# The causal mask of the diagonal score blocks: a minimum on VectorE behind the exponential in place of a matmul ahead of it

## The chip, the cores and the metric

The kernel runs on one core of a Trainium2 chip. The metric is the device time of one execution in microseconds (us); before the change it is 3023.98 us, the median of three runs (3017.05 to 3034.43). The engines are named as in the profile: PE is TensorE's matmuls, PEld its weight loads, DVE is VectorE, ACT is ScalarE, POOL is GpSimd, SP the engine that issues most DMAs. Each engine works through its own queue in order; between engines, semaphores hold an instruction until what it needs is there.

## The reference

One inference step of a small hybrid decoder: a recurrent layer, one shared set of keys, values and log-forget sums, then an attention layer. It is computed for a prompt of 2048 new tokens and, with a paged cache, for 8 sequences of 8 tokens each ("decode" below). The change touches the prompt's attention alone, with 16 heads of 64:

```python
def fox_block(q, k, v, cq, ck, q_pos, k_pos):
    s = jnp.einsum('bqhd,bkhd->bhqk', q, k).astype(jnp.float32) * (HEAD_DIM ** -0.5)
    s = s + jnp.swapaxes(cq, 1, 2)[:, :, :, None] - jnp.swapaxes(ck, 1, 2)[:, :, None, :]
    mask = k_pos[None, :] <= q_pos[:, None]
    s = jnp.where(mask[None, None], s, -jnp.inf)
    p = jax.nn.softmax(s, axis=-1)
    return jnp.einsum('bhqk,bkhd->bqhd', p.astype(v.dtype), v)
```

A key that comes after the query must get the weight zero.

## The kernel before, in words

The program goes through the recurrent layer, the projections, the prompt's attention and the output projection. The attention (from about 1757 to 2825 us in the profile) runs beside most of the decode sequences, whose cached keys and values come in by DMA; the two are interleaved by a fixed share of estimated costs (`Side.along`).

The attention's work is cut into 64 units: a head and a block of 512 queries (`units`, four query blocks `qc` for each of 16 heads). A unit has 4(qc+1) score blocks, each with 128 keys (on the partitions) by 512 queries. For each score block:

- Two matmuls write the scores into a PSUM bank `st`: one with `ka` (L1592), one with `kbt` (L1593), which also brings in the forget sums and the row maximum.
- The last four blocks of a unit lie on the diagonal. Queries ahead of the block's keys are left out (`lo`), and the first 128 remaining columns need a triangular mask. Before the change a third matmul adds it (L1595): the identity in bfloat16 as weights (`identB`) by a fixed tile that holds 0 and -1e30 (`causal`).
- ACT takes the exponential into an SBUF tile (L1601), `acc` for a unit's first block and `p` for the others. There are 5 `acc` and 6 `p` tiles.

After every four blocks a group of product matmuls multiplies these tiles with the values (`product`, L1612, into `ops`). It is called two score blocks later (`later.after(2, product)`), and its first matmul is tied to the last entry of `pair`, the last of the four exponentials (`together`). POOL then adds each `p` to `acc` (line L108, a helper that many operations share), from which the row sums come; a `p` tile is free again when its product matmuls and this addition have read it.

The row maximum for a unit is worked out some units ahead: PE computes the scores once more into one of three banks `sx` (L1431), DVE takes their maximum (L1433; on the diagonal L1435, with a mask tile `maskb`) and frees the bank, PE transposes the maxima (`mps`, L1448), ACT writes them into `qbt` (L1450). DVE also transposes the decode's keys (`ktr`, L1180) and works on decode scores. Decode's matmuls are `dS` (L1148) and `dO` (L1262).

The code's order is not the order of the queues. The layer that builds the program places each instruction in its engine's queue by its own estimate of times, so removing or adding an instruction can move others.

Of the kernel before, what the change touches and what calls it, by code (L numbers as in the profile page):

```python
# [11 lines left out]
F32 = mybir.dt.float32  # L12
F32R = mybir.dt.float32r
I32 = mybir.dt.int32
AF = mybir.ActivationFunctionType
ALU = mybir.AluOpType
# [4 lines left out]
P = 128  # L21
# [10 lines left out]
NEG = -1.0e30  # L32
# [55 lines left out]
def tile_hawk_fox(  # L88
# [8 lines left out]
    V, A, G, T, S = nc.vector, nc.scalar, nc.gpsimd, nc.tensor, nc.sync  # L97
# [9 lines left out]
    def tt(eng, out, a, b, op):  # L107
        eng.tensor_tensor(out, a, b, op=op)  # L108
# [12 lines left out]
    def together(mms, after=(), beside=False):  # L121

        first = mms[0]().ins
        for d in after:
            tc.add_manual_dep(first, d.ins.name, SYNC)
        if beside:
            behind("T", first)
        with tc.high_priority(), tc.issue_after(first):
            for mm in mms[1:]:
                mm()  # L130
# [66 lines left out]
    def ct(name, shape, dtype=F32):  # L197
        return const.tile(shape, dtype, name=name, tag=name)

    ident = ct("ident", [P, P])  # L200
# [21 lines left out]
    def sbuf(es, name, side=None):  # L222
        return es.enter_context(tc.tile_pool(name=name, bufs=1, side=side, reuse_waits="tile"))
# [1110 lines left out]
    def attention(es):  # L1334
        pool = sbuf(es, "att")
# [15 lines left out]
        for i in range(NQ):  # L1351
            if i % 3 == 0 and i < 6:
                kb = kbs[i // 3]
                G.memset(f(kb[64:P, :]), 0.0)
                G.memset(f(kb[96:100, :]), 1.0)
            qb = qbs[i]
            G.memset(f(qb[64:P, :]), 0.0)
            G.memset(f(qb[64:67, :]), 1.0)
            if i == 0:
                G.memset(maskb[:, :], 0.0)  # L1360
                G.affine_select(maskb[:, :], maskb[:, :], pattern=[[-1, 512]], compare_op=ALU.is_ge, fill=NEG, base=384,
                                channel_multiplier=1)

        identB, causal = (pool.tile([P, P], mybir.dt.bfloat16, name=n) for n in ("identB", "causal"))
        V.tensor_copy(identB[:, :], ident[:, :])
        G.memset(causal[:, :], 0.0)
        G.affine_select(causal[:, :], causal[:, :], pattern=[[1, P]], compare_op=ALU.is_ge, fill=NEG, base=0,
                        channel_multiplier=-1)

        sel = pool.tile([P, 4, P], F32R, name="sel16")  # L1370
        rr = pool.tile([P, 512], F32R, name="r16")
# [23 lines left out]
        def load_keys(h):  # L1395
            kb = kbs[h % 2]
            loaded.add(h)
            for lo, hi in halves(h):
                queue[0].dma_start(f(kb[0:64, lo:hi]), kd_d[h * HD:(h + 1) * HD, 1, lo:hi])
                queue[0].dma_start(f(kb[64:67, lo:hi]), nc_d[h, :, lo:hi])  # L1400
# [55 lines left out]
        def finish(u, ops, acc):  # L1456
            h, qc = units[u]
            pr, h2 = divmod(h, 2)
            if u % 8 == 0:
                oTs_["sums"] = pool.tile([P, 32], F32, name="sums", tag="sums", bufs=2)  # L1460
            sums = oTs_["sums"]
            if h2 == 0:
                oTs_[qc] = pool.tile([P, 512], F32, name="oT", tag="oT", bufs=5)
            oT = oTs_[qc][h2 * HD:(h2 + 1) * HD, :].rearrange("d (a r c) -> d a r c", a=2, r=2)
            for r in range(2):
                A.copy(oT[:, :, r, :], ops[r * HD:(r + 1) * HD, :].rearrange("d (a c) -> d a c", a=2))
            accs.append((qc, acc))
            if len(accs) == 4 or h == H - 1:
                later.after(2, lambda todo=accs[:]: total(h2, sums, todo, h >= H - 2))
                accs.clear()  # L1470
            if u >= len(units) - 4:
                later.after(5, lambda oT=[oTs_[qc]]: norm(pr, sums, qc, 1, oT))
            elif u % 8 == 7:
                later.after(5, lambda oT=[oTs_[c] for c in range(4)]: norm(pr, sums, 0, 4, oT))
# [54 lines left out]
        start = [sum(nks[:u]) for u in range(len(units))]  # L1529
        done = [0, 0, 0]  # L1530

        def advance(tick):

            need = 0
            for u in range(len(units)):
                need = max(need, start[u] + nks[u] - 2 * max(0, start[u] - min(LEAD, RAMP + tick) - tick))
                if start[u] > tick + 40:
                    break
            while done[0] < min(need, len(tasks)):
                u, j, ck = tasks[done[0]]  # L1540
                while done[1] <= min(u + 1, len(units) - 1):
                    load_unit(done[1])
                    done[1] += 1
                top(u, j, ck)
                done[0] += 1
# [12 lines left out]
        pair = []  # L1558
        wide = [0]

        def scores_bank():

            if dec_done:
                wide[0] += 1
                if wide[0] % 2:
                    return psum["dec"].tile([P, 512], F32, name="st", tag="do"[wide[0] // 2 % 2], bufs=1)
            return ps3.tile([P, 512], F32, name="st", tag="st", bufs=2)
# [3 lines left out]
        def loads():  # L1571
            while lows[0] < len(units):
                v = lows[0]
                if tick < (start[v - 2] if v < 4 else min(max(start[v - 2], start[v - 3] + AFT), start[v] - 3)):
                    break
                with paged():
                    load_low(v)
                lows[0] += 1
            h, k = divmod(tick, 40)
            if k == 16 and h + 1 < H:  # L1580
                with paged():
                    load_head(h + 1)

        for u, (h, qc) in enumerate(units):
            for k in range(nks[u]):
                loads()
                ka, kb = heads[h], kbs[h % 2]
                qa, qb = qas[u], qbs[u % NQ]
                lo = max(0, k - qc * 4) * P
                ks = slice(k * P, (k + 1) * P)  # L1590
                ps = scores_bank()
                place["T"] = T.matmul(ps[:, lo:], ka[:, ks], qa[:, lo:], start=True, stop=False).ins  # L1592
                T.matmul(ps[:, lo:], kb[:, ks], qb[:, lo:], start=False, stop=(k < qc * 4))  # L1593
                if k >= qc * 4:
                    T.matmul(ps[:, lo:lo + P], identB[:, :], causal[:, :], start=False, stop=True)  # L1595
                done[2] = u + (k == nks[u] - 1)
                if k == 0:
                    p = acc = pool.tile([P, 512], F32, name="acc", tag="acc", bufs=NACC)
                else:
                    p = pool.tile([P, 512], F32, name="p", tag="p", bufs=NP)  # L1600
                pair.append((k, lo, p, A.activation(p[:, lo:], ps[:, lo:], AF.Exp)))  # L1601

                def product(u=u, h=h, todo=pair, acc=acc, last=(k == nks[u] - 1)):


                    nonlocal ops
                    if todo[0][0] == 0:
                        ops = ops2[:, u % 2 * 256:u % 2 * 256 + 256]

                    def mm(k, lo, p, r):  # L1610
                        a0 = (lo // P + 1 - r) // 2
                        return T.matmul(ops[r * HD:(r + 1) * HD, a0 * P:], vvs[h % 2][:, k, :],  # L1612
                                        p[:, :].rearrange("p (a r c) -> p a r c", a=2, r=2)[:, a0:, r, :],
                                        start=(k == 0), stop=(last and k == todo[-1][0] - 1 + r))

                    together([partial(mm, k, lo, p, r) for k, lo, p, _ in todo for r in range(2) if lo <= (2 + r) * P],
                             [todo[-1][3]])
                    for k, lo, p, _ in todo:
                        if k:
                            tt(a_l(), acc[:, lo:], acc[:, lo:], p[:, lo:], ALU.add)  # L1620
                    if last:
                        finish(u, ops, acc)

                if k % 4 == 3:
                    later.after(2, product)
                    pair = []
                before = done[0]
                advance(tick)
                tick += 1
                later.tick()  # L1630
                if k + sum(nks[u - u % 4:u]) == 0 and h + 1 < H:
                    load_keys(h + 1)
                yield 4.1 * (512 - lo) * 0.42 + (done[0] - before) * 213
# [224 lines left out]
    psum["att"] = banks(att, "psa", 6)  # L1858
    cost = sum(4.1 * 0.42 * (512 - max(0, k - qc * 4) * P) + 213 for qc in range(4) for k in range(4 * qc + 4)) * H
    side.along(attention(att), ((16 - FIRST) * TURN - side.spent) / (cost * SPAN))  # L1860
    place.clear()
    side.upto(1e12)
# [38 lines left out]
```

## Time and profile before

| | |
|---|---|
| median of 3 runs | 3023.98 us (3017.05 to 3034.43) |
| the profiled execution | 3028.43 us, of which 3026.4 us lie between its first and last instruction |
| granted TensorE clock, mean | 0.969 of full speed |
| PE, PEld busy | 2803.4 us (93%), 2252.1 us (74%) |
| DVE, ACT, POOL busy | 1805.5 us (60%), 1269.9 us (42%), 1084.4 us (36%) |
| causal matmuls (L1595) | 256, from 1756.8 to 2824.2 us |
| exponentials (L1601) | 640, from 1757.4 to 2824.8 us |
| product matmuls (L1612) | 2432 in the trace, where each of the program's stands as two, from 1762.4 to 2871.4 us |

Rows of the profile read `line engine operation out<-in shape xcount | busy us, mean ns | idle before it, and what ended that`. Rows of a timeline read `start, length in us, engine, line, operation, xcount [idle before it]`; equal neighbours are merged into one row. A matmul's length is a model and overlaps the next; the distance from start to start tells what it holds up. Rows of waits read `who waits <- for whom: total us, times, longest`.

### The profile page before, as it was taken

The numbers are of one execution on the slowest core, as the hardware profiler recorded it, in microseconds if no ns is written. First come the engines' busy times: TensorE is split into PE (matmuls) and PEld (weight loads), VectorE is DVE, ScalarE is ACT, GpSimd is POOL, SyncE is SP. The second block draws the span as 40 slices with busy tenths as digits, with TensorE's granted clock in tenths as the row PEclk, the third lists the DMA queues.
The fourth block names the chain that finished last, engine by engine and source line by source line (L and its number), as shares of the span: only waits on it lengthen the run. The fifth ranks groups of instructions, "written<-read, shape, count | busy, mean of one in ns | idle before, by whom it ended". The sixth has DMA issues, their size and how long they took to land.

```text
span 3026.4 us, 60467 instructions
## 1 busy us (share of the span) xinstructions
PE 2803.4 (93%) x21614; PEld 2252.1 (74%) x21614; DVE 1805.5 (60%) x4012; ACT 1269.9 (42%) x2874; POOL 1084.4 (36%) x1199
## 2 busy tenths in 40 slices
PE   6998999998997999999999699998998999999998
PEld 5997789988887997888889556665665666565687
DVE  6877455425427775676564466656776756655344
ACT  4665342222125665534333234444544444355321
POOL 1653201000002653100000245665575656659422
PEclk9999999999998999999999889999999999999999
DMA  4224546888863226699999968898899888874343
GB/s 123 79 88 133 171 126 191 256 263 281 278 216 91 89 88 194 209 313 338 332 346 326 279 209 243 248 282 255 250 291 287 267 251 265 260 247 122 98 145 110
DMA packets 479103, 653.79 MB, mean 216 GB/s; under 512 B 91291, under 2 KB 277020, under 8 KB 471525
## 3 DMA queue, kind: packets, MB, share of 16 engines
q1 hardware_dynamic: 475174, 644.26, 67.4%
q10 hardware_dynamic: 3340, 3.56, 0.4%
q8 instruction: 171, 2.80, 0.4%
q0 software_dynamic: 288, 2.10, 0.2%
q14 instruction: 130, 1.06, 0.1%
HBM read 514.22 MB, written 135.16 MB: 215 GB/s over the span
## 4 chain that ended last, share of the span: by engine, by line
PE 59%; DMA 16%; DVE 9%; ACT 6%; SPq 5%; issue 3%; POOL 1%; ACTq 0%; DVEq 0%; POOLq 0%
PE ops L1612 7%; PE st L1592 4%; PE y L383 4%; PE y L384 4%; PE y L385 4%; DMA raw<-in_cache_k_dram 4%; PE sx L1431 4%; PE dO L1262 3%; DMA raw<-in_cache_v_dram 3%; PE st L1593 3%; PE dS L1148 3%; PE kv L383 3%; PE kv L385 3%; PE kv L384 3%; SPq L1093 2%
## 5 line engine op out<-in xcount | busy, mean ns | idle before, releaser
L108 POOL TENSOR_TENSOR acc<-acc,p 128x512 f32<-128x512 f32 (+3 forms) x576 | 640.9, 1114 | 347.7 <-PE ops L1612 211.2
L1601 ACT ACTIVATE p<-st 128x512 f32<-128x512 f32 (+3 forms) x576 | 291.3, 525 | 400.1 <-PE st L1593 177.5
L1180 DVE STREAM_TRANSPOSE ktr<-raw 128x1024 f32<-128x1024 f32 x256 | 308.2, 1226 | 125.1 <-DMA raw<-in_cache_k_dram 116.5
L1433 DVE TENSOR_REDUCE mxs<-sx 128x1 f32<-128x512 f32 x384 | 255.0, 681 | 141.0 <-PE sx L1431 139.6
L383 PE MATMUL kv<-wh,xh 128*128 128x256 f32 (+3 forms) x1088 | 310.0, 288 | 6.4 <-ACT wh L427 4.7
L384 PE MATMUL kv<-wl,xh 128*128 128x256 f32 (+3 forms) x1088 | 309.3, 287 | 5.7 <-DVE wl L428 5.7
L385 PE MATMUL kv<-wh,xl 128*128 128x256 f32 (+3 forms) x1088 | 309.6, 286 | 2.7 <-DMA xl<-xld 2.7
L1592 PE MATMUL st<-qa,ka 128*128 128x512 f32 (+3 forms) x640 | 269.9, 422 | 13.3 <-ACT p L1601 7.5
L1612 PE MATMUL ops<-p,vvt 128*64 128x256 f32 (+1 forms) x2176 | 262.9, 369 | 1.0 <-ACT p L1601 0.7
L1431 PE MATMUL sx<-kbt,qbt 96*128 96x512 f32 (+3 forms) x640 | 229.2, 416 | 29.9 <-DMA qbt<-qd 24.2
L1113 POOL TENSOR_TENSOR qw<-qb,amask 128x128 f32<-128x128 f32 x64 | 29.1, 460 | 618.1 <-PE dS L1148 325.3
L428 DVE SCALAR_TENSOR_TENSOR wl<-wst,gv,wh 128x256 fp32r<-128x256 f32 (+1 forms) x384 | 169.4, 504 | 131.8 <-ACT wh L427 131.5
L427 ACT ACTIVATE wh<-wst,gv 128x256 fp32r<-128x256 f32 (+1 forms) x384 | 164.6, 499 | 190.2 <-DMA wst<-in_w_kv_dram 72.7
L1593 PE MATMUL st<-qbt,kbt 128*128 128x512 f32 (+3 forms) x640 | 236.9, 370 | 0.0
L383 PE MATMUL qg<-xh,wh 128*128 128x512 f32 (+2 forms) x640 | 229.4, 359 | 0.0
L384 PE MATMUL qg<-xl,wh 128*128 128x512 f32 (+2 forms) x640 | 228.2, 357 | 0.0
L385 PE MATMUL qg<-xh,wl 128*128 128x512 f32 (+2 forms) x640 | 227.5, 356 | 0.6 <-DVE wl L428 0.6
L1612 PEld LDWEIGHTS ops<-p,vvt 128*64 128x64 f32 x2176 | 161.5, 141 | 88.2 <-issue 19.8
L383 PEld LDWEIGHTS kv<-wh,xh 128*128 128x128 f32 (+1 forms) x1088 | 203.5, 188 | 13.2 <-ACT wh L427 6.8
L384 PEld LDWEIGHTS kv<-wl,xh 128*128 128x128 f32 (+1 forms) x1088 | 203.2, 188 | 10.1 <-DVE wl L428 6.9
L385 PEld LDWEIGHTS kv<-wh,xl 128*128 128x128 f32 (+1 forms) x1088 | 204.8, 188 | 7.0 <-issue 3.7
L1592 PEld LDWEIGHTS st<-qa,ka 128*128 128x128 f32 x640 | 123.7, 193 | 112.8 <-issue 54.4
(297 smaller groups left out, 6356.3 us busy)
## 6 DMA issues: line engine op xcount, KB each, us to landing
raw<-in_cache_k_dram SPq DMA_DIRECT2D x512, 256.0 KB
raw<-in_cache_v_dram SPq DMA_DIRECT2D x512, 256.0 KB
wst<-in_w_kv_dram SPq DMA_DIRECT2D x48, 512.0 KB
wst<-in_b_w_in_dram SPq DMA_DIRECT2D x48, 512.0 KB
xt<-in_x_prompt_dram SPq DMA_DIRECT2D x32, 512.0 KB
wst<-in_a_w_in_dram SPq DMA_DIRECT2D x64, 256.0 KB
out_dram<-kf SPq DMA_DIRECT2D x128, 128.0 KB
sc<-cd SPq DMA_DIRECT2D x16, 1024.0 KB
```

The source lines that it names most:

```text
L108: eng.tensor_tensor(out, a, b, op=op)
L383: T.matmul(ps, lh(k), rh(k), start=(k == 0), stop=False)
L384: T.matmul(ps, lh(k), rl(k), start=False, stop=False)
L385: T.matmul(ps, ll(k), rh(k), start=False, stop=(k == nk - 1))
L428: V.scalar_tensor_tensor(wl[:, k, :], st[:, k, :], gk, f(wh[:, k, :]), op0=ALU.mult, op1=ALU.subtract)
L1180: behind("V", V.transpose(t.kts[pp][:, n], raw[:, :, pp * 256:(pp + 1) * 256]).ins)
L1431: T.matmul(ps[:, :w], qb[0:96, j * P:(j + 1) * P], kb[0:96, ck * 512:ck * 512 + w], start=True, stop=True)
L1433: place["V"] = V.reduce_max(mx[:, j, ck:ck + 1], ps[:, :w], axis=AX.X).ins
L1592: place["T"] = T.matmul(ps[:, lo:], ka[:, ks], qa[:, lo:], start=True, stop=False).ins
L1593: T.matmul(ps[:, lo:], kb[:, ks], qb[:, lo:], start=False, stop=(k < qc * 4))
L1601: pair.append((k, lo, p, A.activation(p[:, lo:], ps[:, lo:], AF.Exp)))
L1612: return T.matmul(ops[r * HD:(r + 1) * HD, a0 * P:], vvs[h % 2][:, k, :], p[:, :].rearrange("p (a r c) -> p a r c", a=2, r=2)[:, a0:, r, : ...
```

## The change

The mask moves behind the exponential. The third matmul is gone, the second closes the accumulation. The exponential now runs over unmasked scores in the triangle as well, where it may give large values or infinity. Behind it DVE takes the minimum, in place, of the first 128 columns and a fixed tile `cap` that holds 3e38 where the key is allowed and 0 where it is not: allowed weights stay, the others become 0. `pair` now holds this minimum in place of the exponential, so a unit's last product is tied to the fourth minimum. `cap` is in float32 and takes the place of the two bfloat16 tiles and of the cast that made one of them.

```diff
-        identB, causal = (pool.tile([P, P], mybir.dt.bfloat16, name=n) for n in ("identB", "causal"))
-        V.tensor_copy(identB[:, :], ident[:, :])
-        G.memset(causal[:, :], 0.0)
-        G.affine_select(causal[:, :], causal[:, :], pattern=[[1, P]], compare_op=ALU.is_ge, fill=NEG, base=0,
-                        channel_multiplier=-1)
+        cap = pool.tile([P, P], F32, name="cap")
+        G.memset(cap[:, :], 3e38)
+        G.affine_select(cap[:, :], cap[:, :], pattern=[[1, P]], compare_op=ALU.is_ge, fill=0.0, base=0, channel_multiplier=-1)
...
-                T.matmul(ps[:, lo:], kb[:, ks], qb[:, lo:], start=False, stop=(k < qc * 4))
-                if k >= qc * 4:
-                    T.matmul(ps[:, lo:lo + P], identB[:, :], causal[:, :], start=False, stop=True)
+                T.matmul(ps[:, lo:], kb[:, ks], qb[:, lo:], start=False, stop=True)
...
-                pair.append((k, lo, p, A.activation(p[:, lo:], ps[:, lo:], AF.Exp)))
+                came = A.activation(p[:, lo:], ps[:, lo:], AF.Exp)
+                if k >= qc * 4:
+                    came = V.tensor_tensor(p[:, lo:lo + P], p[:, lo:lo + P], cap[:, :], op=ALU.min)
+                pair.append((k, lo, p, came))
```

The queues differ from 1757 us on. One place shows how: the last unit of head 2 (query block 3), around its last diagonal block and its last product. PE before, from the last diagonal block's score matmuls to the start of the product (a row's end gives the shape and how often it stands there):

```order
L1592 MATMUL st<-qa,ka 128x128
L1593 MATMUL st<-qbt_19868,kbt_19862 128x128
L1595 LDWEIGHTS identB
L1595 MATMUL st<-causal,identB 128x128
L1592 MATMUL st<-qa,ka 128x512
L1431 MATMUL sx<-kbt_19870,qbt_19864 128x512
L1431 MATMUL sx<-kbt_19870,qbt_19864 128x128
L1593 MATMUL st<-qbt_19863,kbt_19870 128x512
L1612 MATMUL ops<-p,vvt_19859 64x256 x2
L1612 MATMUL ops<-p,vvt_19859 64x128
```

PE at the same place now (line numbers are those of the changed kernel: L1590 and L1591 are the score matmuls, L1429 is sx, L1611 the product):

```order
L1590 MATMUL st<-qa,ka 128x128
L1591 MATMUL st<-qbt_19868,kbt_19862 128x128
L1590 MATMUL st<-qa,ka 128x512
L1429 MATMUL sx<-kbt_19870,qbt_19864 128x512
L1429 MATMUL sx<-kbt_19870,qbt_19864 128x128
L1591 MATMUL st<-qbt_19863,kbt_19870 128x512
L1590 MATMUL st<-qa,ka 128x512
L1591 MATMUL st<-qbt_19863,kbt_19870 128x512
L1429 MATMUL sx<-kbt_19870,qbt_19864 128x512
L1611 MATMUL ops<-p,vvt_19859 64x256 x2
L1611 MATMUL ops<-p,vvt_19859 64x128
```

The mask's weight load and matmul are gone, and a second score block and one more sx matmul now stand between the last diagonal block and the product.

DVE before, at the same place (oTs and sgt belong to decode's and the attention's outputs, mrow holds the maxima that PE transposes):

```order
L1444 TENSOR_REDUCE mrow_19900<-mxs 128x4
L108 TENSOR_TENSOR oTs<-dres,drb 64x4x8 x2
L108 TENSOR_TENSOR sgt<-sgt,rp 128x512
L1433 TENSOR_REDUCE mxs<-sx 128x1 x2
L1180 STREAM_TRANSPOSE ktr<-raw 128x1024
```

and now (L1599 is the minimum, L1442, L1431 and L1180 are the old L1444, L1433 and L1180):

```order
L1599 TENSOR_TENSOR p<-p,cap 128x128
L1442 TENSOR_REDUCE mrow_19896<-mxs 128x4
L1599 TENSOR_TENSOR p<-p,cap 128x128 x2
L108 TENSOR_TENSOR oTs<-dres,drb 64x4x8 x2
L108 TENSOR_TENSOR sgt<-sgt,rp 128x512
L1431 TENSOR_REDUCE mxs<-sx 128x1
L1599 TENSOR_TENSOR p<-p,cap 128x128
L1431 TENSOR_REDUCE mxs<-sx 128x1
L1180 STREAM_TRANSPOSE ktr<-raw 128x1024
```

The four minima of the unit stand between DVE's other rows, which keep their order; the fourth, for which the product waits, stands behind sgt and one maximum.

## The prediction

> **What bounds the kernel now.** I read the page's head first, then the busy time of each engine over the stretch in which the diagonal score blocks run, then single rows around one such block.
>
> ```profile
> span 3026.4 us, 60467 instructions
> PE 2803.4 (93%) x21614; PEld 2252.1 (74%) x21614; DVE 1805.5 (60%) x4012; ACT 1269.9 (42%) x2874; POOL 1084.4 (36%) x1199
> ```
>
> The busy times by stretch (columns: stretch, length, busy us of PE, PEld, DVE, ACT, POOL with instruction counts, granted clock, DMA share, GB/s):
>
> ```profile
> core 0: us, PE busy (x) PEld busy (x) DVE busy (x) ACT busy (x) POOL busy (x), PEclk, DMA share, GB/s
> 1690.00:1757.00 67.00, 38.33 (x201) 26.94 (x192) 25.91 (x66) 11.12 (x35) 17.02 (x27) 0.73 0.82 238
> 1757.00:2825.00 1068.00, 1004.99 (x8835) 641.27 (x8834) 682.99 (x1432) 500.45 (x1215) 685.09 (x641) 0.97 0.79 244
> 1757.00:2700.00 943.00, 887.34 (x8098) 568.03 (x8096) 618.12 (x1310) 427.81 (x1059) 583.86 (x556) 0.97 0.84 259
> 2700.00:2825.00 125.00, 117.65 (x739) 73.23 (x739) 64.87 (x122) 72.65 (x156) 101.23 (x85) 1.00 0.45 136
> ```
>
> All 256 diagonal blocks lie in 1757 to 2825. There PE is busy 1005 of 1068 us (94%), DVE 683 (64%), POOL 685 (64%), ACT 500. So PE sets the pace and DVE looks as if it had room. Decode ends near 2700; in the last 125 us POOL is busy 101 (81%). The rest of the program does not change: its instructions stand in the same order.
>
> **The change, part by part.** *Removed: 256 causal matmuls on PE.*
>
> ```profile
> L1595 PE MATMUL st<-causal,identB x256: 229/230/330, 1756.8 to 2824.2; 128*128 128x128 bf16 x128
> ```
>
> Their 230 ns is a modelled duration that overlaps the next matmul; 256 x 0.23 = 59 us is not what they cost. The cost is what the next starts lose. With one (PE's timeline):
>
> ```profile
> 2766.63 0.39 PE L1593 MATMUL st<-qbt,kbt 128*128 128x512 f32 x1
> 2766.86 0.23 PE L1595 MATMUL st<-causal,identB 128*128 128x128 bf16 x1
> 2766.90 0.48 PE L1431 MATMUL sx<-kbt,qbt 96*128 96x512 f32 x1
> 2767.22 0.34 PE L1592 MATMUL st<-qa,ka 128*128 128x384 f32 x1
> ...
> 2400.50 0.39 PE L1593 MATMUL st<-qbt,kbt 128*128 128x512 f32 x1
> 2400.73 0.23 PE L1595 MATMUL st<-causal,identB 128*128 128x128 bf16 x1
> ...
> 2402.77 0.44 PE L1592 MATMUL st<-qa,ka 128*128 128x384 f32 x1
> ```
>
> and without one, the same neighbours:
>
> ```profile
> 2217.74 0.39 PE L1593 MATMUL st<-qbt,kbt 128*128 128x512 f32 x1
> 2217.96 0.40 PE L1431 MATMUL sx<-kbt,qbt 96*128 96x512 f32 x1
> 2218.20 0.39 PE L1592 MATMUL st<-qa,ka 128*128 128x512 f32 x1
> ...
> 2491.16 0.40 PE L1593 MATMUL st<-qbt,kbt 128*128 128x512 f32 x1
> ...
> 2493.37 0.50 PE L1592 MATMUL st<-qa,ka 128*128 128x512 f32 x1
> ```
>
> From L1593 over one sx matmul to the next L1592 it takes 0.59 us with and 0.46 without: 0.13. Over a product of 16 it takes 2.27 and 2.21: 0.06. The step over the causal matmul alone is 0.04 (2766.86 to 2766.90), and that is the floor: 10 us in all; 0.13 everywhere would be 33. Score and sx matmuls follow about twice as often as anything else, so I take 0.11: **-28 us**, between -33 and -10.
>
> *Added: 256 minima of 128x128 on DVE, both inputs in SBUF.* The trace has no such operation. Nearest by size is the masked maximum of 128x128, nearest by operands are two small TENSOR_TENSOR between SBUF tiles in the same stretch (minimum/median/maximum):
>
> ```profile
> L1435 DVE CUSTOM_DVE_ANT_0 sx<-sx,maskb 128x128 f32<-128x128 f32 x56 | 16.0, 286 | 31.8 <-PE sx L1431 31.5
> ...
> L108 DVE TENSOR_TENSOR dss<-dss x9: 113/907/1225, 1842.3 to 2665.6; 8x8 f32<-8x8 f32 x9
> L108 DVE TENSOR_TENSOR ddg<-dss,qmask x9: 170/346/1168, 1843.5 to 2666.5; 128x64 f32<-128x64 f32 x9
> ```
>
> The 8x8 takes 0.11 us at best, 0.91 in the median and 1.23 at most. What it waits for while it counts as busy is a POOL instruction:
>
> ```profile
> L108 POOL TENSOR_TENSOR acc<-acc,p 128x512 f32<-128x512 f32 (+3 forms) x576 | 640.9, 1114 | 347.7 <-PE ops L1612 211.2 <-ACT p L1601 92.5 <-ACT sc L1217 5.8
> ```
>
> An addition takes 1.11 us and POOL is busy 64% of the stretch; 0.64 x half of 1.11 = 0.36 us of waiting on average, between the medians' surplus of 0.18 (ddg) and 0.79 (dss). So a minimum costs 0.29 + 0.36 = 0.65 us, 166 us in all, and DVE goes from 683 to 849 of 1068 (80%), if PE's pace stays.
>
> [...]
>
> *Where that lies on PE's path: the last product of a unit.* It now waits for the unit's fourth minimum, not for its fourth exponential. Between last diagonal block and product, PE's order gains one score block and one sx matmul; in DVE's queue the fourth minimum stands behind the two oTs products, the sgt product and one maximum. The same place before (the unit of head 2, last query block; timelines of PE, ACT, DVE, POOL):
>
> ```profile
> 1961.69 0.45 PE L1593 MATMUL st<-qbt,kbt 128*128 128x512 f32 x1
> 1962.07 1.52 PE L1612 MATMUL ops<-p,vvt 128*64 128x256 f32 x14
> ...
> 1961.39 0.28 ACT L1601 ACTIVATE p<-st 128x128 f32<-128x128 f32 x1
> ...
> 1960.55 0.69 DVE L108 TENSOR_TENSOR sgt<-sgt,rp 128x512 f32<-128x512 f32 x1
> 1961.15 1.37 DVE L1433 TENSOR_REDUCE mxs<-sx 128x1 f32<-128x512 f32 x2
> ...
> 1957.21 7.22 POOL L108 TENSOR_TENSOR acc<-acc,p 128x512 f32<-128x512 f32 x6
> ```
>
> The exponential ends at 1961.67, the first of the two maxima at 1961.84 (half of 1.37 later than 1961.15). A minimum could start there, is 0.29 long and has POOL adding without a break: done at 2.13 + a wait of 0 to 1.2, say 1962.49. The product stood at 1962.07; take off 0.33 for three causal matmuls, add 0.70 for the new block and sx matmul (three starts 0.23 apart): 1962.44. So the extra work in front of the product just covers the minimum without POOL, and what POOL's additions add, 0.36 us on average, is left over. 64 units: **+23 us**, between 0 (more cover elsewhere) and 64 x 1.11 = 71 (a full addition each time).
>
> *Smaller terms.* Each has a row:
>
> ```profile
> ACT p L1601 <- POOL acc L108: 38.1, 34, 3.5
> PEld sx L1431 <- DVE mxs L1433: 8.5, 19, 1.1
> PEld sx L1431 <- DVE mxs L1435: 6.5, 14, 1.0
> ```
>
> Behind each minimum in DVE's queue stand maxima that free the three sx banks. PE's loads wait 15 us for them at a DVE load of 64%; with busy over idle going from 1.8 to 4, I take as much again: **+13** (0 to 26). A later product holds the p tiles longer; ACT waits 38 us for them now, of which some reaches PE: **+10** (0 to 38). In the last 125 us some 40 minima of 0.29 meet a POOL that is 81% busy: **+4** (0 to 12). The fixed tile replaces two tiles and a cast ahead of the stretch, where POOL is busy 17 of 67 us: 0, at worst under 1 without that cover. The exponentials of the diagonal start some 0.1 us earlier; ACT is half idle, so nothing.
>
> Sum: -28 + 23 + 13 + 10 + 4 = +22. The profiled execution took 3028.4 us (span and start), 4.4 above the median of the three runs; 3050 for it, **3046 us** against the median of 3024.
>
> **The rivals.** *Gain kept (ends on the other side).* The minima hide because the new order gives each unit's last product enough work in front. Place: that product; if its extra wait stays under 0.1 us (6 us in all) and the smaller terms are nearly nothing, 3024 - 28 + 4 = 3000. It decides in favour of faster as soon as all losses together stay under 13 us, 0.2 per unit. For it: DVE is idle a third of the time, and its own order is unchanged but for the minima. Against it: the 0.91 us median of an 8x8 operation.
>
> *Break-even.* The product waits 0.36 but banks and p tiles cost nothing: -28 + 23 + 4, about 3023.
>
> *DVE becomes a second bound.* At 80% and more, in a queue that waits on ACT, sx banks come late in every unit. One more wait of 0.7 us (a maximum) per unit is 45 us on top of the 22: 3091.
>
> *PE is not what limits the stretch.* Then the matmuls cost nothing (the change does not do what it says) and only the losses stay: 3024 + 50 = 3074. For it: DMA is busy 84% until 2700. Against it: starts 0.23 apart wherever no wait is shown. [...] The 0.13 us between the two pairs speaks against it.
>
> **How the numbers follow.** Forecast (slower by up to 2%) 0.33, DVE a second bound 0.08, PE not the limit 0.06: slower by over 0.5% 0.47. Break-even, within 0.5% (15 us, about what the runs' spread of 3017 to 3034 lets one tell): 0.29. Gain kept: 0.24. The range runs from 3000 (the first rival) to 3088 (the forecast, with the wait at the products twice over, 23 more, and 19 of what the bounds of banks and p tiles leave open); the forecast's own is 3039 to 3080.
>
> **What would show it.** Right: no L1595; a 128x128 TENSOR_TENSOR on DVE with a mean of 0.5 to 0.8 us and a minimum near 0.25; PE waiting on it before products (some 20 us in all); DVE at 75 to 82% of the stretch. Start to start from the second score matmul over one sx matmul near 0.46 throughout. Wrong: a mean near 0.3 (no contention with POOL), or hardly any wait of PE on the minimum, means the gain is kept; sx matmuls waiting on DVE for 40 us or more means the DVE rival.

## The result, and the profile after

The changed kernel takes 3049.34 us (median of 6 runs, 3041.72 to 3051.83), the kernel before, run beside it, 3026.66 (6 runs, 3017.05 to 3036.67). The ratio is 1.0058, with a 95% interval of 1.0034 to 1.0083: 10 to 25 us slower. Below, a difference in us is the difference of two such ratios times 3027 us.

The page's head and the busy times by stretch, with the columns known from before:

```profile
span 3045.4 us, 60178 instructions
PE 2792.7 (92%) x21358; PEld 2238.8 (74%) x21358; DVE 1914.5 (63%) x4267; ACT 1267.4 (42%) x2874; POOL 1085.4 (36%) x1199
...
1757.00:2845.00 1088.00, 999.99 (x8577) 633.60 (x8576) 789.29 (x1684) 496.64 (x1212) 687.42 (x641) 0.96 0.78 240
```

and the same stretch of the kernel before:

```profile
1757.00:2845.00 1088.00, 1024.99 (x8918) 654.29 (x8917) 689.58 (x1454) 504.10 (x1223) 690.35 (x646) 0.97 0.78 241
```

PE is busy 25 us less, and the stretch ends later all the same; DVE is at 73%. The minima and POOL's additions of the changed kernel (one line's instructions, shortest, median and longest in ns; then the group rows, with busy us and mean ns):

```profile
L1599 DVE TENSOR_TENSOR p<-p,cap x240: 237/291/1406, 1759.3 to 2848.5; 128x128 f32<-128x128 f32 x120
...
L1599 DVE TENSOR_TENSOR p<-p,cap 128x128 f32<-128x128 f32 x240 | 122.3, 525 | 33.2 <-ACT p L1597 32.8
...
L108 POOL TENSOR_TENSOR acc<-acc,p 128x512 f32<-128x512 f32 (+3 forms) x576 | 642.2, 1116 | 361.9 <-PE ops L1611 210.2 <-ACT p L1597 61.5 <-DVE p L1599 57.0
```

A minimum takes 0.24 us at best and 0.52 on average (0.525 for the 240 on p, 0.46 for the 16 on acc). In the trace, 131 of the 256 begin while POOL runs an instruction and take 0.75 us on average; the other 125 take 0.28, none over 0.30. Of the 131, 128 end after the POOL instruction that ran as they began, at the median 0.15 us after it. POOL is held up too, but hardly: 40 additions begin while a minimum runs that had found POOL idle. The 27 of them with at least 0.18 us of that minimum still to go take 0.12 us longer than additions of the same shape that meet no minimum, the other 13 no longer. That is 3 us in all, so the mean over the 576 stays at 1.116 us, before 1.114.

What PE and its weight loads wait for, in the changed kernel (total us, times, longest; a PE row and a PEld row are largely the same stops, seen twice: each of PE's 122 here lies in one of PEld's):

```profile
PE st L1590 <- ACT p L1597: 18.9, 40, 1.3
PE dO L1262 <- DMA raw<-in_cache_v_dram: 17.6, 10, 4.1
PE sx L1429 <- DVE mxs L1431: 11.6, 14, 3.7
PE ops L1611 <- DVE p L1599: 10.1, 12, 1.8
...
PEld sx L1429 <- DVE mxs L1431: 26.1, 44, 4.0
PEld ops L1611 <- DVE p L1599: 17.3, 20, 2.1
PEld sx L1429 <- DVE mxs L1433: 11.0, 22, 2.6
```

and in the kernel before:

```profile
PE dO L1262 <- DMA raw<-in_cache_v_dram: 19.4, 13, 3.1
PE rp L1505 <- DMA r<-rs: 11.5, 6, 4.2
PE st L1592 <- ACT p L1601: 7.5, 20, 0.8
...
PE sx L1431 <- DVE mxs L1435: 2.6, 5, 0.7
```

The waits that the prediction named are all there: products for a minimum, score blocks for a p tile, sx for the maxima. Whether the minima cause them is another question: the change also moved rows in TensorE's queue all along the stretch, and a moved row can wait on its own account.

### The profile page after: what moved, and what is told of

It is laid out like the page before. It is cut to its first block, busy times and chain, and to the rows that moved or that the text cites. A ratio compares the mean times of both kernels' runs of the same rounds, so it can differ in the third digit from the quotient of the medians.

```text
span 3045.4 us, 60178 instructions
## 1 busy us (share of the span) xinstructions
PE 2792.7 (92%) x21358; PEld 2238.8 (74%) x21358; DVE 1914.5 (63%) x4267; ACT 1267.4 (42%) x2874; POOL 1085.4 (36%) x1199
## 4 chain that ended last, share of the span: by engine, by line
PE 45%; DMA 18%; DVE 9%; ACT 4%; SPq 3%; issue 3%; POOL 2%; ACTq 0%; DVEq 0%; POOLq 0%
PE ops L1611 6%; DMA raw<-in_cache_k_dram 4%; PE st L1590 3%; PE sx L1429 3%; PE dO L1262 3%; PE y L383 3%; PE y L384 3%; PE y L385 3%; PE dS L1148 3%; PE st L1591 2%; DMA raw<-in_cache_v_dram 2%; PE kv L383 2%; PE kv L384 2%; PE kv L385 2%; SPq L1093 2%
## 5 line engine op out<-in xcount | busy, mean ns | idle before, releaser
L1180 DVE STREAM_TRANSPOSE ktr<-raw 128x1024 f32<-128x1024 f32 x256 | 307.8, 1225 | 134.6 <-DMA raw<-in_cache_k_dram 118.0
L1431 DVE TENSOR_REDUCE mxs<-sx 128x1 f32<-128x512 f32 x384 | 255.6, 679 | 112.9 <-PE sx L1429 111.9
L1590 PE MATMUL st<-qa,ka 128*128 128x512 f32 (+3 forms) x640 | 263.1, 414 | 26.4 <-ACT p L1597 18.9
L1611 PE MATMUL ops<-p,vvt 128*64 128x256 f32 (+1 forms) x2176 | 263.2, 368 | 11.6 <-DVE p L1599 10.1
L1429 PE MATMUL sx<-kbt,qbt 96*128 96x512 f32 (+3 forms) x640 | 226.6, 414 | 48.7 <-DMA qbt<-qd 26.4
L1611 PEld LDWEIGHTS ops<-p,vvt 128*64 128x64 f32 x2176 | 162.4, 141 | 100.8 <-issue 18.5
L1591 PE MATMUL st<-qbt,kbt 128*128 128x512 f32 (+3 forms) x640 | 234.3, 370 | 0.0
L1590 PEld LDWEIGHTS st<-qa,ka 128*128 128x128 f32 x640 | 122.8, 192 | 126.0 <-ACT p L1597 59.1
```

Of the source, the lines that this page charges most:

```text
L1180: behind("V", V.transpose(t.kts[pp][:, n], raw[:, :, pp * 256:(pp + 1) * 256]).ins)
L1429: T.matmul(ps[:, :w], qb[0:96, j * P:(j + 1) * P], kb[0:96, ck * 512:ck * 512 + w], start=True, stop=True)
L1431: place["V"] = V.reduce_max(mx[:, j, ck:ck + 1], ps[:, :w], axis=AX.X).ins
```

## The experiments: first each operation by itself

Four kernels take the matmul or the minimum away or put both in, and leave the order of the queues to the building layer.

**Neither matmul nor minimum** (the mask is left out):

```diff
-                if k >= qc * 4:
-                    came = V.tensor_tensor(p[:, lo:lo + P], p[:, lo:lo + P], cap[:, :], op=ALU.min)
```

> The changed kernel with its minimum left out as well, so that diagonal blocks aren't masked at all (the output of the attention is wrong for it; nothing else is left out). Theory (PE limits the stretch, the causal matmuls cost it 28 us, the minima take this back and more): 2999 us, 2992 to 3010, with the 15 us of PE's waits on sx banks back near the level before. Rival (PE isn't the limit of the stretch, so the matmuls cost nothing): 3020 to 3030. Rival (the order that the building layer makes without the matmul is what costs): 3035 or more.

Measured: 3035.86 us, ratio 1.0045 (1.0029 to 1.0061), 14 us slower than before. With less work on PE and none added anywhere, no term of the prediction gives a loss. Only the order is left as a cause.

**The fourth block's mask as a matmul, the first three as minima:**

```diff
-                T.matmul(ps[:, lo:], kb[:, ks], qb[:, lo:], start=False, stop=True)
+                tri = k == qc * 4 + 3
+                T.matmul(ps[:, lo:], kb[:, ks], qb[:, lo:], start=False, stop=not tri)
+                if tri:
+                    T.matmul(ps[:, lo:lo + P], identB[:, :], causal[:, :], start=False, stop=True)
...
-                if k >= qc * 4:
+                if qc * 4 <= k < qc * 4 + 3:
```

> Minimum for the first three diagonal blocks of a unit, the causal matmul again for the fourth, on whose weights the last product waits (the fixed tile of the minimum is in bfloat16 here, for room). Theory (the product's wait on the fourth minimum is the largest loss): three quarters of the 28 us stay, the 27 us of PE waiting on minima before products nearly vanish, 3020 to 3032 us. Rival (the load of the minima on DVE is what costs, wherever they stand): three quarters of the loss stay, 3040 to 3046.

Measured: 3056.63 us, ratio 1.0118 (1.0098 to 1.0138): slower than the changed kernel, and outside both expectations (3020 to 3032, 3040 to 3046). A miss for both; the order of the queues, which is not held here, may be why.

**Matmul and minimum for every diagonal block** (the kernel before, with the minimum added):

> Causal matmul and minimum, both for all diagonal blocks: the minimum added and nothing taken away (fixed tile in bfloat16, for room). Theory (PE limits, the matmuls cost 28 us): 3049 + 28 = 3077 us, 3065 to 3085. Rival (the matmuls cost nothing): 3045 to 3055.

Measured: 3075.3 us, ratio 1.0159 (1.0137 to 1.0180). It came as expected, but the four corners do not add up: the minima cost 48 us beside the matmuls (1.0159 against 1) and 4 us without them (1.0058 against 1.0045), while the matmuls cost 31 us beside the minima and minus 14 without. Two prices that depend so much on one another are not prices of the operations.

**One input in place of two** (the mask is left out: DVE reads the 128x128 block of p and writes one column elsewhere):

```diff
-                    came = V.tensor_tensor(p[:, lo:lo + P], p[:, lo:lo + P], cap[:, :], op=ALU.min)
+                    came = V.reduce_max(junk[:, :], p[:, lo:lo + P], axis=AX.X)
```

> In place of the minimum a maximum over the same 128x128, which reads one SBUF tile and writes one column: DVE is busy about as long and the last product waits for it, but it has a single SBUF input (the mask is left out). Theory (a good part of the loss is the minima's wait for POOL, 0.52 us on average against 0.28 without): the operation takes 0.25 to 0.30 us throughout, DVE loses some 60 us of busy time, PE's wait on it before products falls from 27 to 10 us, 3022 to 3036 us. Rival (the place in the queue costs, not its length): 3043 to 3050.

Measured: 3030.34 us, ratio 1.0025 (1.0007 to 1.0043). It lies as expected, 10 us below the changed kernel. But its order is its own, so the 10 us cannot be put down to the second input. What it does show is the operation's length (shortest, median and longest in ns):

```profile
L1600 DVE TENSOR_REDUCE junk<-p x240: 222/282/289, 1755.4 to 2820.7; 128x1 f32<-128x128 f32 x120
```

With one SBUF input none takes longer than 0.29 us, although 171 of the 256 begin while POOL runs an instruction. A minimum, with two, took up to 1.4.

## The experiments: the order held fixed

So the next kernels fix the order. Two strike instructions out of the finished queues; the others build the program twice, read from the first build in which order each engine's instructions stand, and bind the second build to it:

```diff
+    order = built(inputs, True)[2]
+    return built(inputs, False, order)[:2]
...
+        for e in (order or ()):
+            line = [made[e][x] for x in order[e]]
+            for x, y in zip(line, line[1:]):
+                tc.add_manual_dep(y, x.name, ORDER)
```

In the traces of the three kernels below that keep all minima and bind TensorE, all its 21358 matmuls other than the mask's stand in the sequence of the kernel before.

**The old order without the matmuls:**

> The kernel before, with its 256 causal matmuls and their weight loads struck out of the finished queues; what each signalled, the instruction of TensorE ahead of it signals now, and all else stands in the order of the kernel before, row by row (the mask is left out, which the output shows). Theory A, that the matmuls lie on the path with some 28 us and that e1_no_mask (3036) lost this and more by the other order that the building layer gave it: 2998, between 2990 and 3008. Theory B, that TensorE's time for them is no part of the path, whatever the order: 3020 to 3030.

Measured: 3013.06 us, ratio 0.9956 (0.9937 to 0.9975). So the matmuls are worth 13 us (8 to 19): half of theory A's 28, and more than theory B's nothing. The time lies between the two expected ranges.

**The new order without the minima.** What follows a struck minimum on VectorE still waits for what POOL had to have done by then; the readers of the tile wait for the exponential.

> The changed kernel, with its 256 minima struck out of VectorE's finished queue; who reads such a p tile waits for the exponential in their place, and all else stands in the order of the changed kernel (the mask is left out). It executes the same instructions as x1_no_mask_old_order, only in another order, so the two differ by the order alone, and the changed kernel differs from this one by the minima alone. If the minima are the loss (+50 us by the terms of the prediction, its matmuls' share put back): 2995 to 3005. If the order is (e1_no_mask, again another order, took 3036): 3025 to 3040, and the minima are worth only 10 to 25 us.

Measured: 3037.22 us, ratio 1.0027 (1.0010 to 1.0044). This kernel executes the same instructions as the one above it. The order alone therefore costs 0.0071, 21 us, and the minima in the changed kernel 0.0031, 9 us (the two intervals overlap, so the 9 are small rather than known). PE's and PEld's waits in the old order:

```profile
PE st L1592 <- ACT p L1601: 7.9, 22, 0.8
...
PEld st L1592 <- ACT p L1601: 43.9, 102, 1.2
...
PEld sx L1431 <- DVE mxs L1433: 8.7, 23, 1.1
```

and in the new one, without a single minimum:

```profile
PE st L1590 <- ACT p L1597: 19.9, 39, 1.4
PE dO L1262 <- DMA raw<-in_cache_v_dram: 19.6, 11, 4.0
PE sx L1429 <- DVE mxs L1431: 9.8, 12, 3.1
...
PEld st L1590 <- ACT p L1597: 61.9, 118, 1.5
...
PEld sx L1429 <- DVE mxs L1431: 21.9, 35, 3.4
PEld sx L1429 <- DVE mxs L1433: 9.6, 19, 2.0
```

The longer waits for p tiles and for the maxima are those of the changed kernel (18.9 and 11.6 us on PE). They come with the order, not with the minima.

**The minima in the old order** (all four engines bound):

> The changed kernel, with TensorE, VectorE, ScalarE and POOL held to the order of the kernel before; only the minima are put in, where the building layer finds them a place. If the loss is the minima's own: 3045 to 3055, as the changed kernel (3049). If a good part of the loss is the order: 3008 to 3030, which would be x1_no_mask_old_order and the price of the minima, 10 to 30 us.

Measured: 3117.01 us, ratio 1.0308 (1.0289 to 1.0327). Neither theory had this. Against the old order without mask the minima cost 0.0352, 107 us. The changed kernel, with the building layer's own order, is 0.0250, 76 us, faster than this one. The waits of PE:

```profile
PE ops L1621 <- DVE p L1609: 104.9, 51, 5.4
PE dO L1263 <- DMA raw<-in_cache_v_dram: 11.7, 9, 3.3
PE st L1598 <- ACT p L1607: 6.3, 19, 0.8
```

The products wait at 51 places, 2.06 us each. One of them, in PE's timeline:

```profile
1997.32 0.39 PE L1599 MATMUL st<-qbt,kbt 128*128 128x512 f32 x1
2002.86 1.55 PE L1621 MATMUL ops<-p,vvt 128*64 128x256 f32 x7 [5.15 <-DVE p L1609]
```

and in DVE's over the same time:

```profile
1997.46 1.24 DVE L1181 STREAM_TRANSPOSE ktr<-raw 128x1024 f32<-128x1024 f32 x1
1998.62 0.54 DVE L1441 CUSTOM_DVE_ANT_0 sx<-sx,maskb 128x384 f32<-128x384 f32 x1
1999.07 0.14 DVE L1441 DVE_READ_ACCUMULATOR2_ANT mxs<- 128x1 f32 x1
1999.07 0.69 DVE L1439 TENSOR_REDUCE mxs<-sx 128x1 f32<-128x512 f32 x1
1999.67 1.24 DVE L1181 STREAM_TRANSPOSE ktr<-raw 128x1024 f32<-128x1024 f32 x1
2000.84 0.64 DVE L1155 TENSOR_REDUCE gmx<-sc 128x4 f32<-128x512 f32 x1
2001.40 1.23 DVE L1181 STREAM_TRANSPOSE ktr<-raw 128x1024 f32<-128x1024 f32 x1
2002.56 0.25 DVE L1609 TENSOR_TENSOR p<-p,cap 128x128 f32<-128x128 f32 x1
```

The minimum itself takes 0.25 us. It stands behind three transposes of decode's keys and three reductions, 5 us of DVE's own work, and the product behind it has nothing in front that would fill the time.

**Both masks in the old order:**

> Matmul and minimum for every diagonal block (cap in bf16), held to the order of the kernel before. Against f1_minima_old_order it prices the matmuls beside the minima: 28 us if TensorE is the limit in both, under 10 us if TensorE waits for the minima anyway. Against the kernel before it prices the minima beside the matmuls. If both prices add up at a fixed order, this is f1 + 28, 3040 to 3055 with a loss by order in the changed kernel, 3070 to 3080 without; e3_both in its own order took 3075.

Measured: 3131.92 us, ratio 1.0350 (1.0337 to 1.0364), 0.0042 (13 us) above the minima alone and 0.0350 (106 us) above the matmuls alone. At one fixed order the four corners add up: 13 us for the matmuls with or without minima (each known to some 6 or 7 us), 106 or 107 for the minima with or without matmuls. What did not add up in the first four kernels was their order. The 13 us lie between the expectation's 28 (TensorE the limit in both) and 10. The time itself lies above all the ranges that were expected, because the minima alone already took 3117.

**Which queue's order does it, TensorE's alone:**

> The changed kernel with TensorE alone held to the order of the kernel before; VectorE, ScalarE and POOL are ordered by the building layer. f1_minima_old_order, with all four held, took 3117. Theory C, that TensorE's old order sets the products so near behind the exponentials that no minimum fits between: 3095 to 3120, and TensorE waits over 80 us for p from the minima again. Theory D, that f1 lost by VectorE's old order, in which the minima stand behind other work: 3020 to 3055, and that wait falls under 30 us.

Measured: 3135.58 us, ratio 1.0352 (1.0327 to 1.0378), 13 us above the kernel with all four engines bound. The wait is as theory C has it (over 80 us), the time 16 us above its range.

```profile
PE ops L1621 <- DVE p L1609: 104.4, 50, 5.2
```

**VectorE's alone:**

> The changed kernel with VectorE alone held to the order of the kernel before (the minima put in where the building layer finds them a place), TensorE free. Theory C: about the time of the changed kernel, 3040 to 3060. Theory D: 3090 to 3120.

Measured: 3056.99 us, ratio 1.0094 (1.0072 to 1.0116).

```profile
PE ops L1621 <- DVE p L1609: 12.2, 14, 2.3
```

The two kernels speak for theory C: in TensorE's old order the products stand too near behind the exponentials, with VectorE's order bound as well as free. Once TensorE may put more in front of them, as the second score block and the sx matmul at the place shown with the change, the wait is about an eighth.

**Which minima:**

> Minimum for the first three diagonal blocks of a unit, matmul for the fourth (cap in bf16), TensorE held to the order of the kernel before. The second term of the prediction says that the price lies at the fourth minimum, which the unit's last product waits for at once, while the first three have time: then 3015 to 3030 (three quarters of the 14 us of x1_no_mask_old_order gained, little paid). If the first three come late too, as VectorE has other work ahead of them: over 3050, and TensorE's wait for p from the minima stays over 40 us. e2_fourth_by_matmul, the same work in its own order, took 3057.

Measured: 3054.96 us, ratio 1.0078 (1.0052 to 1.0104). The time is that of the second expectation (over 3050), the wait is not (under 40 us):

```profile
PE ops L1620 <- DVE p L1608: 17.8, 19, 2.4
```

Against the kernel with all four minima at the same order of TensorE it is 0.0274, 83 us, faster; with the 3 us that 64 matmuls cost (a quarter of 13), the fourth minima cost 86 us, 1.3 each. The first three cost the remaining 0.0122 against the old order without mask, 37 less 3, so 34 us or 0.18 each. Up to 13 of these may belong to the other engines' orders, which are bound there and free here. The place that the prediction named, the fourth minimum, was right. Its 0.36 us for each was reckoned with more work in front of the product, which TensorE's old order does not have.

**Another order of the kernel before:**

```diff
-SHARE = 1.13
+SHARE = 1.12
```

> The kernel before with one number of its planner changed, SHARE from 1.13 to 1.12; the mask is as before, and no instruction is added or removed, but 1762 of TensorE's 12052 rows stand elsewhere. If the orders are about equal: 3017 to 3037. If the kernel before has an order that others seldom match (the order of the changed kernel costs 24 us by y0 against x1): 3040 to 3055.

Measured: 3021.03 us, ratio 0.9977 (0.9961 to 0.9992). Moving 1762 rows of TensorE costs nothing, so it isn't that any order but the old one is bad. It is even the fastest kernel with a mask here, by 7 us (2 to 12).

## Why the prediction was right in the sum, and where its steps were not

The forecast of 3046 us, slower by over half a per cent, came about: 3049, though the lower end of the interval (1.0034) is under that half per cent. The sum of +22 hit 18 by luck: two errors and a missing term nearly cancel. In the prediction's groups: removed -28, added +50. By the runs: matmuls -13, order +21, minima in the order as built +9. These are prices along one path, which takes away the matmuls, then changes the order, then adds the minima. With the minima added in the old order they cost 107, and the new order then saves 76: the sum is the same, but order and minima have no prices of their own.

- **"So I take 0.11: -28 us."** Measured 13 us (8 to 19) at both corners, 0.05 per matmul. The price on PE itself was right. Laid side by side, the traces of the kernel before and of the same order without the matmuls differ by 0.10 us over the three starts behind L1593, on average of the 208 places where PE does not wait in them (0.11 where a score or sx matmul follows, 0.08 elsewhere), and a score or sx matmul follows 177 of the 256. The step that failed is to carry this price to the kernel's time in full. In these two executions PE is busy 24 us less between the first and the last exponential, but idle 8 us more (71 us against 63), so the stretch is 17 us shorter: waits for something else take part of the gain back. The two executions as a whole are 22 us apart, the medians 13 to 14; I go by the timed runs, and what makes up the rest stays open. That PE's time counts at all, against the rival in which PE is not the limit, the old order without the matmuls shows.
- **"A minimum costs 0.29 + 0.36 = 0.65 us."** Measured 0.52, of which 0.24 at best; DVE 73% instead of 80, just under the 75 to 82 that were to show the forecast right. That it waits for a POOL instruction was right, the wait too large by 0.13. In the kernel before, 13 of the 18 dss and ddg operations of the stretch begin beside a POOL addition, and each ends 0.015 to 0.08 us after it. In the changed kernel a minimum takes 0.75 us beside POOL and 0.28 without; the operation with one input takes 0.28 in the median and never over 0.29. POOL in its turn loses only 3 us in all by the minima, under 1 of them in the last 125 us.
- **"The last product of a unit: +23."** In the order as built, which the term was made for, PE waits 10.1 us at 12 places. The prediction read the new rows in front of the product as cover, which is what the bound kernels show them to be. The step that failed is to charge POOL's average wait at all 64 products: at most of them the cover takes it away. Without that cover, in the old order of TensorE, the fourth minima cost 86 us, beyond the upper bound of 71, since there up to 5 us of VectorE's queue stand in front of the minimum and not one addition of POOL.
- **"sx banks late: +13"** and **"p tiles held longer: +10."** PEld's wait for the maxima went from 15.0 to 37.1 us, PE's for p from 7.5 to 18.9. That is 22 and 11 us more. Sizes and places fit roughly, the cause does not: without any minimum, in the same order, they are 31.5 and 19.9 us.
- **"In the last 125 us: +4."** From the last exponential of unit 55 (2721 us) to that of unit 63 the changed kernel takes 112.4 us and the kernel before 103.4, 9 more. The new order without the minima loses 5 there against the old one without the matmuls (108.4 and 103.0). The term was too small, and most of it is the order.
- **The step that was missing:** the order had been used only as cover in front of the product and had no price of its own. Without the minima it costs 21 us.
- **The rivals.** "Gain kept" would have needed the old order's 13 us and minima that hide; they hide only in the new order. In its favour the prediction said that DVE's own order is unchanged but for the minima. That holds at the place it showed; over the whole trace up to some 230 of DVE's 4012 instructions stand elsewhere. DVE is no second bound at 73%: PEld's wait for the maxima, 37.1 us, stays just under the 40 that were to show it, and most of it is there without a minimum. Break-even, at 3023, lies outside the interval.

What stays open is why the new order costs 21 us. In the two profiled executions without a mask, the stretch from the first to the last exponential is 32 us longer in the new order (1082.8 and 1050.9); PE is idle 11 us more in it, and slower clock, by the estimate of the last section, accounts for up to 15. What in the order brings this on is not shown. To make room for the minima cannot be the whole reason: the kernel with neither mask had no minima when it was ordered, and is 0.0089, 27 us, slower than the same instructions in the old order. But the old order isn't singular either, as the other SHARE shows. Both bad orders were made without the matmuls; whether this matters, or chance, no run tells. Nor is it shown that there is no order that keeps the 13 us and hides the minima.

## What to carry to other kernels

The operation that replaced another in a different engine's queue was priced here by what stood ahead of it in that queue, and by what the waiting engine had to do meanwhile: 0.25 us of work cost 1.3 us at the tight place and little (9 us over 256 minima) in an order with more matmuls in between. Where a scheduler makes the order, single experiments mix an operation's price with that of a new order; at a bound order the prices of these four kernels added up. A sum of terms that comes out right is no proof of its terms.

## What the runs showed of the hardware

In the kernel with the minima in the old order, a wait of PE was followed by a spell at half the granted clock. PE waits 2.13 us for a minimum, and half a microsecond after it goes on, the clock falls to 0.51. The wait in PE's timeline:

```profile
2470.89 2.30 PE L1621 MATMUL ops<-p,vvt 128*64 128x256 f32 x14 [2.13 <-DVE p L1609]
```

and the same microseconds by stretch (the column behind POOL's is the granted clock):

```profile
2468.80:2470.90 2.10, 0.01 (x1) 0.01 (x2) 2.10 (x5) 0.02 (x1) 1.73 (x2) 1.00 1.05 387
2470.90:2471.40 0.50, 0.50 (x6) 0.35 (x8) 0.50 (x3) 0.00 (x0) 0.42 (x1) 1.00 1.04 381
2471.40:2474.80 3.40, 3.40 (x16) 2.37 (x12) 1.67 (x2) 1.09 (x3) 0.04 (x1) 0.51 0.47 140
2474.80:2477.00 2.20, 2.20 (x38) 1.12 (x41) 0.41 (x1) 0.84 (x2) 0.00 (x0) 0.98 0.77 259
```

In that spell three score matmuls of 128x512 start 0.42 and 0.43 us apart (2473.72, 2474.14, 2474.57); just ahead of the wait a matmul follows one of that size by 0.23 (2467.29, 2467.52). By that I estimate that 3.4 us at 0.51 lose 1.7 us, on top of the 2.13. Over the attention this trace has 25 such spells, 18 of about 3.4 us and 7 of about 6.8, and 23 of them begin within 4 us of a wait of over 1 us. Not every wait is followed by one: of six between 2 and 2.5 us, four were. That the waits bring the spells on is read from this nearness alone. The span and the mean granted clock over the whole execution, in the old order without mask:

```profile
core 0: 3004.5 us, clock 0.971
```

in the new order without mask:

```profile
core 0: 3035.0 us, clock 0.965
```

and with the minima in the old order:

```profile
core 0: 3110.3 us, clock 0.960
```

I estimate the clock's loss as 1 less this share, times the time: 87, 106 and 124 us. Between these three executions that makes up to 37 us for the minima in the old order, and up to 19 for the new order. Over all executions of each kernel (7, 12 and 5) the mean losses are 91, 101 and 127 us: of the 107 us that the minima cost in the old order up to 36 are clock, of the 21 us of the new order only up to 10 (at most, as the estimate counts slow spells also where PE stands still: from 2000 to 2002 us in the kernel with the minima in the old order PE has no busy time, and the clock is 0.61). The prediction had no such term, though the 0.97 stood in its rows.
